# The samples' paged-cache attention as a third stream inside prompt attention

## Chip, cores and metric

One core of one Trainium2 chip. The metric is device time in microseconds of one execution, the median of three runs.

## The reference

One inference step of a two-layer decoder trunk: a gated-DeltaNet layer with a ConvFFN, then a multi-head latent attention (MLA) layer with a ConvFFN. The step serves a prompt of 1040 tokens (16 learned meta tokens and 1024 tokens) and eight samples with one new token each. The second layer keeps one shared latent key/value row of 256 numbers and one rotated positional key of 64 numbers per token. A prompt token attends causally to the prompt. A sample attends to its own 4096 cached tokens, which lie in pages of 128 tokens in a pool, and to its own new token:

```python
def latent_scores(q_lat, q_pe, c, k_rope):
    s = jnp.einsum('bqhr,bkr->bhqk', q_lat, c) + jnp.einsum('bqhd,bkd->bhqk', q_pe, k_rope)
    return s.astype(jnp.float32) * MLA_SCALE

def sample_attend(q_lat, q_pe, c, k_rope, c_past, k_past):
    ...
    s_past = latent_scores(q_lat, q_pe, c_past, k_past)
    ...
    prob = jax.nn.softmax(jnp.concatenate([s_past, s_new], axis=-1), axis=-1).astype(c.dtype)
    return (jnp.einsum('bhqk,bkr->bqhr', prob[..., :P], c_past)
            + jnp.einsum('bhqk,bkr->bqhr', prob[..., P:], c))
```

After attention each head's latent result is multiplied by `w_uv`, all heads go through the output projection `b_w_out`, and a norm and the last ConvFFN follow. There are eight heads; all data is float32.

## The kernel before

Activations lie transposed, with features on partitions and the 1048 tokens along the free dimension: the eight samples first, then the prompt, in chunks of 280, 384 and 384 columns (`CH`). Products of the trunk are taken three times over halves of a split float32 number (`mm3`, L226). Products written directly in float32 take two matmul records each in the profile.

Code is written as generators that yield a position. `merge` (L834) runs those of one stage in order of position, which gives the program order; the framework under it then settles, ahead of the run, the order of the instructions on each engine and on the DMA queue that SyncE issues (SP's queue), by program order and its own estimate of times. On the chip every queue runs strictly in that order, and an instruction that waits holds up what is behind it.

Three stages matter here.

**Latents** (to L1227). `lat_qa` makes `qah` and `qal`, the two halves of the low-rank query, with a row factor kept in `RQ`.

**Prompt attention** (L1230 to L1440). `merge` runs `attend` with one `heads_in` per head. Position h to h+1 is head h. `heads_in` loads and splits that head's weights and makes queries (`q_nope`, `q_rope`, scaled by `RQ` on VectorE, L1279), keys and values; it also makes the samples' query of that head, against transposed `w_uk` (L1261, L1289). `attend` takes nine blocks of 116 queries: `scores` writes to `sc` in PSUM (five products), VectorE masks and takes the maximum (L1365 to L1373), ScalarE takes the exponential (L1375), VectorE scales by the row sum (L1382). `mix` transposes the probabilities on TensorE (L1394), and products with the values `vt` collect in `po` (L1408), which rotates through two PSUM banks and is stored to `og_d` in DRAM.

**Cache attention and output projection** (L1443 to L1616). `merge` runs `cache_all` with `outp`. `cache_unit` runs 16 times, one unit for 2048 cached tokens of one sample. GpSimd gathers two `cg` tiles of 1 MB (L1468) and one `krt` tile (L1471) by indirect DMA. TensorE transposes the latents (L1487) and the positional keys (L1476) into PSUM, VectorE and ScalarE copy them out. Scores come from `ql` and `qr_s` as 32-column weights on four column tiles (L1493) and on 64-row tiles (L1497). Then the maximum (L1502), the exponential (L1506), transposes of the probabilities (L1510), products with `cg` (L1516) and a running rescale of `OS` (L1523 to L1531). `join` merges the partial results, adds the new token, and multiplies by `w_uv` (L1591) and by `b_w_out` for the samples (L1599). `outp` (L300) projects the prompt's columns.

## Time and profile before

| | us |
|---|---|
| median of three runs (lowest 3307.54, highest 3319.37) | 3309.26 |
| the profiled execution | 3314.68 |
| its span, first to last instruction | 3312.9 |
| prompt attention, with the last latents | 1770 to 2150 |
| cache attention, join, output projection | 2150 to 2490 |

The mean granted TensorE clock of the profiled execution is 0.975 of full speed. The page gives the share of the span in which each engine was busy and the chain of work that ended last. A stage is read from the table of stretches, an order from the timeline, a price from the groups of instructions by line and shape. A matmul's duration has a pipeline tail in it: the pace is the distance between starts.

### The profile page before, as it was taken

Reading aid. Unit: us, or ns where it says so; the run is one execution under the profiler, and the core shown is the slowest. Engines: PE = TensorE matmul, PEld = TensorE weight load, DVE = VectorE, ACT = ScalarE, POOL = GpSimd, SP = SyncE. Lnnn points to the kernel's source line nnn. Section 1 sums busy time; section 2 is a strip of 40 time slices with the busy share of each in tenths; the row PEclk is TensorE's granted clock in tenths of the full one; section 3 lists DMA queues with packets and bytes.
Section 4 is the critical chain, followed back from the end, with each engine's and each line's share of the span. In section 5 each row is a group of like instructions: output and inputs, shape, how many; then the busy total and the mean of one; then the engine's idle time right before and its main releaser. Section 6 shows DMA issues by size and latency. Waiting matters only on the chain.

```text
span 3312.9 us, 52527 instructions
## 1 busy us (share of the span) xinstructions
PE 3123.5 (94%) x20846; PEld 2884.2 (87%) x20846; DVE 2030.3 (61%) x4139; ACT 1254.9 (38%) x2541; POOL 862.2 (26%) x1013
## 2 busy tenths in 40 slices
PE   7999999999899999999978999999998999999997
PEld 6888888888799999999967888856678999999996
DVE  4777777766864555555576676544557355555556
ACT  4656555563433222222334444433224322222223
POOL 1433222210342222322342111111105332322322
PEclk9999999999899999999989999999998999999999
DMA  3222222235321111111121000354432111111111
GB/s 107 62 65 69 64 67 59 72 105 176 96 66 46 39 52 49 48 46 39 45 86 44 25 27 28 108 189 184 159 102 84 46 46 45 46 45 52 46 39 66
DMA packets 267650, 235.08 MB, mean 71 GB/s; under 512 B 57919, under 2 KB 246597, under 8 KB 263285
## 3 DMA queue, kind: packets, MB, share of 16 engines
q1 hardware_dynamic: 260224, 189.69, 19.7%
q0 software_dynamic: 6912, 41.95, 3.4%
q8 instruction: 164, 2.69, 0.3%
q14 instruction: 82, 0.66, 0.1%
q10 hardware_dynamic: 268, 0.09, 0.0%
HBM read 198.84 MB, written 33.40 MB: 70 GB/s over the span
## 4 chain that ended last, share of the span: by engine, by line
PE 76%; DVE 14%; DMA 3%; issue 3%; ACT 2%; POOL 1%; SPq 0%; ACTq 0%; POOLq 0%; DVEq 0%
PE fps L228 9%; PE fps L229 9%; PE fps L227 9%; PE fdn L228 5%; PE fdn L227 5%; PE fdn L229 5%; PE psu L227 2%; PE psu L229 2%; PE po L1408 2%; PE psu L228 2%; PE dscr L1493 2%; DVE acc L287 2%; PE psop L227 1%; DVE tm L658 1%; DVE xs L660 1%
## 5 line engine op out<-in xcount | busy, mean ns | idle before, releaser
L144 POOL TENSOR_TENSOR ws<-ws,vec 128x1024 f32<-128x1024 f32 (+1 forms) x127 | 249.5, 1965 | 424.3 <-DMA ws<-in_f_w_up_dram 210.1
L228 PE MATMUL fps<-xfl,wh 128*128 128x384 f32 (+1 forms) x1056 | 343.7, 326 | 8.2 <-POOL xfl L295 8.1
L227 PE MATMUL fps<-xfh,wh 128*128 128x384 f32 (+1 forms) x1056 | 341.8, 324 | 8.0 <-ACT xfh L293 7.0
L228 PE MATMUL fps<-xbl,wh 128*128 128x384 f32 (+1 forms) x1056 | 343.6, 325 | 4.8 <-POOL xbl L295 4.7
L227 PE MATMUL fps<-xbh,wh 128*128 128x384 f32 (+1 forms) x1056 | 341.6, 324 | 1.1 <-ACT xbh L293 0.5
L229 PE MATMUL fps<-xfh,wl 128*128 128x384 f32 (+1 forms) x1056 | 342.4, 324 | 0.0
L229 PE MATMUL fps<-xbh,wl 128*128 128x384 f32 (+1 forms) x1056 | 341.2, 323 | 0.0
L966 DVE TENSOR_TENSOR fu<-fps,RS 128x384 f32<-128x384 f32 x176 | 98.0, 557 | 386.6 <-PE fps L229 386.1
L151 ACT CAST wh<-ws 128x1024 fp32r<-128x1024 f32 (+1 forms) x144 | 148.0, 1027 | 491.6 <-PE fps L228 373.8
L227 PE MATMUL fdn<-gh,dh 128*128 128x384 f32 (+1 forms) x960 | 315.2, 328 | 0.0
L228 PE MATMUL fdn<-gl,dh 128*128 128x384 f32 (+1 forms) x960 | 311.6, 325 | 0.0
L229 PE MATMUL fdn<-gh,dl 128*128 128x384 f32 (+1 forms) x960 | 308.6, 321 | 0.0
L1044 DVE TENSOR_TENSOR acc<-acc,fdn 128x384 f32<-128x384 f32 (+1 forms) x432 | 216.7, 514 | 108.8 <-PE fdn L229 108.0
L227 PE MATMUL psu<-xah,wh 128*128 128x384 f32 (+1 forms) x768 | 261.8, 341 | 9.5 <-ACT u L533 5.1
L228 PE MATMUL psu<-xal,wh 128*128 128x384 f32 (+1 forms) x768 | 260.0, 339 | 0.7 <-DVE xal L223 0.7
L229 PE MATMUL psu<-xah,wl 128*128 128x384 f32 (+1 forms) x768 | 259.0, 337 | 0.7 <-DVE wl L152 0.7
L975 DVE SCALAR_TENSOR_TENSOR fy<-fu,fcv,fy 128x1064 f32<-128x1064 f32 x176 | 238.6, 1357 | 7.6 <-ACT fy L973 7.3
L152 DVE TENSOR_TENSOR wl<-ws,wh 128x1024 fp32r<-128x1024 f32 (+1 forms) x144 | 173.6, 1206 | 71.3 <-ACT wh L151 71.1
L228 PEld LDWEIGHTS fps<-xfl,wh 128*128 128x128 f32 x1056 | 200.7, 190 | 10.8 <-POOL xfl L295 10.5
L227 PEld LDWEIGHTS fps<-xfh,wh 128*128 128x128 f32 x1056 | 200.3, 190 | 9.4 <-ACT xfh L293 7.9
L228 PEld LDWEIGHTS fps<-xbl,wh 128*128 128x128 f32 x1056 | 200.5, 190 | 6.9 <-POOL xbl L295 6.5
L227 PEld LDWEIGHTS fps<-xbh,wh 128*128 128x128 f32 x1056 | 200.2, 190 | 1.7 <-ACT xbh L293 0.9
(963 smaller groups left out, 7856.1 us busy)
## 6 DMA issues: line engine op xcount, KB each, us to landing
ws<-in_f_w_up_dram SPq DMA_DIRECT2D x88, 512.0 KB
ds<-in_f_w_down_dram SPq DMA_DIRECT2D x44, 512.0 KB
ws<-in_a_w_in_dram SPq DMA_DIRECT2D x32, 512.0 KB
xt<-in_x_prompt_dram SPq DMA_DIRECT2D x16, 512.0 KB
of<-og_d SPq DMA_DIRECT2D x32, 192.0 KB
xr<-x_d SPq DMA_DIRECT2D x16, 384.0 KB
GC<-gcd SPq DMA_DIRECT2D x24, 174.0 KB
Ss<-in_state_delta_S_dram SPq DMA_DIRECT2D x8, 512.0 KB
```

Of the source, the lines that this page charges most:

```text
L144: G.tensor_tensor(st, st, bc(fo, [P, kt, m]), op=ALU.mult)
L151: A.copy(hi, st)
L152: V.tensor_tensor(lo, st, hi, op=ALU.subtract)
L227: PE.matmul(ps, wh, ah, start=start, stop=False)
L228: PE.matmul(ps, wh, al, start=False, stop=False)
L229: PE.matmul(ps, wl, ah, start=False, stop=stop)
L287: V.scalar_tensor_tensor(a_[:, k + j, :], a_[:, k + j, :], vc(wname, k + j), res[j], op0=ALU.mult, op1=ALU.add)
L966: V.tensor_tensor(u[:, 18 + t0:18 + t0 + n], ps[:, :n], RS[:, t0:t0 + n], op=ALU.mult)
L975: V.scalar_tensor_tensor(y, u[:, j:j + LW], fcv[:, l, j, tl:tl + 1], y, op0=ALU.mult, op1=ALU.add)
L1044: V.tensor_tensor(acc[c][:, m, :], acc[c][:, m, :], ps[:, :n], op=ALU.add)
L1408: PE.matmul(po[:, :nq], vt[:kk, kb, P * (h % 2):P * (h % 2) + P], pT[:kk, j, :nq], start=(kb == 0), stop=(kb == i))
L1493: PE.matmul(sc[32 * j:32 * j + 32, :], ql[:, k, b, :], cT[:, j, :], start=(k == 0), stop=False, tile_position=(0, 32 * j))
```

## The change

The whole cache attention and the join move into the merge of prompt attention, as further streams; the output projection runs alone behind it and takes the samples' columns too, since the join now stores them to `og_d`.

- A unit is now 1024 cached tokens (32 units), spread evenly over positions `C0` = 0.15 to `C1` = 7.2, each with its steps at 0, 0.1, 0.25, 1.1, 1.35 and 1.55 unit lengths. Unit n+2 is gathered after unit n's last product: there are two `cg` buffers, two `cT`, two `cB`.
- No TensorE transposes of the cache. VectorE transposes 32 by 32 blocks (`turned`), SyncE stores the tile to DRAM and reads it back in four transfers, each into 32 partitions.
- Scores have 256 columns each instead of 512; the positional part contracts over all 128 partitions, with half of `qr_s` zero.
- The samples' queries are made once for all heads (`sample_queries`), with the queries as 32-column weights.
- `RQ` is folded into `qah` and `qal` in `lat_qa`; VectorE's product L1279 goes, and the subtraction for `qnl` moves from GpSimd to VectorE.
- The scaling of the probabilities (L1382) moves from VectorE to GpSimd.
- Fewer buffers: P 3 to 2, pT 4 to 3; `po` becomes four slots of one PSUM bank; the scores and products of the cache share one bank (`halves`).

The core of the diff:

```diff
-PTB = 4
+PTB = 3
+PB = 2
+C0 = 0.15
+C1 = 7.2
...
         def lat_qa(c):
             t0, n = CH[c]
-            stat(kst, [acc[c][:, 3 + m, :] for m in range(3)], n, RQ[:, t0:t0 + n], QL)
+            r = utile("rqa")
+            stat(kst, [acc[c][:, 3 + m, :] for m in range(3)], n, r[:, :n], QL)
             for m in range(3):
                 a = acc[c][:, 3 + m, :]
-                A.activation(qah[:, m, t0:t0 + n], a, AF.Copy, scale=vc("b_qa", m))
-                V.scalar_tensor_tensor(qal[:, m, t0:t0 + n], a, vc("b_qa", m), qah[:, m, t0:t0 + n], op0=ALU.mult, op1=ALU.subtract)
+                V.scalar_tensor_tensor(a, a, vc("b_qa", m), r[:, :n], op0=ALU.mult, op1=ALU.mult)
+                A.copy(qah[:, m, t0:t0 + n], a)
+                G.tensor_tensor(qal[:, m, t0:t0 + n], a, qah[:, m, t0:t0 + n], op=ALU.subtract)
...
-                u = atile("qu")
-                V.tensor_tensor(u[:, :n], ps[:, :n], RQ[:, t0:t0 + n], op=ALU.mult)
-                return u[:, :n], t0, n
+                return ps[:, :n], t0, n
...
-                G.tensor_tensor(hd["qnl"][:, t0:t0 + n], u, hd["qnh"][:, t0:t0 + n], op=ALU.subtract)
+                V.tensor_tensor(hd["qnl"][:, t0:t0 + n], ps, hd["qnh"][:, t0:t0 + n], op=ALU.subtract)
...
-                V.tensor_scalar(pp[:nq, :nk], pp[:nq, :nk], ls[:nq, 0:1], None, op0=ALU.mult)
+                G.tensor_scalar(pp[:nq, :nk], pp[:nq, :nk], ls[:nq, 0:1], None, op0=ALU.mult)
...
+        def fetch(n):
+            if n < 4 * NS:
+                fetched[n] = big("cg")
+                G.indirect_dma_start(fetched[n], None, crows, offset(n))
...
+        def turned(src, tmp, nb, nm):
+
+            V.transpose(grid(tmp, nb, 8, 32), src.rearrange("p i (b r) -> p b i r", r=32))
+            d = dp.tile([P, nb, 256], F32, tag=nm, name=nm, bufs=2)
+            SP.dma_start(d, grid(tmp, nb, 256))
+            return d.rearrange("(q r) b c -> b r q c", q=4)
+
+        def cache_unit(n, at_):
+
+            b, g = divmod(n, 4)
+            yield at_(0.0)
...
+            src = turned(grid(fetched.pop(("r", n)), 8, ROPE), cpg.tile([P, 1024], F32, tag="cB", name="krB")[:, :512], 2, "krd")
+            for i in range(2):
+                for f in range(2):
+                    SP.dma_start(krT[64 * f + 32 * i:64 * f + 32 * i + 32, :].rearrange("r (q c) -> r q c", q=2), src[i, :, f:4:2, :])
+            fetch_r(n + 1)
+            cT = []
+            for k in range(2):
+                yield at_(0.1 + 0.15 * k)
+                t = cmat("cT")
+                cT.append(grid(t, 4, 256))
+                src = turned(c8[:, :, P * k:P * k + P], cpg.tile([P, 1024], F32, tag="cB", name="cB"), 4, "cBd")
                 for i in range(4):
-                    PE.transpose(pt[:, P * i:P * i + P], krt[:, P * (4 * gg + i):P * (4 * gg + i) + P], ident)
-                V.tensor_copy(krT[:, gg, :], pt)
...
+                    SP.dma_start(cT[k][32 * i:32 * i + 32], src[i])
+            yield at_(1.1)
+            sc = halves[:, 0, :]
             for k in range(2):
...
                 for j in range(4):
-                    PE.matmul(sc[32 * j:32 * j + 32, :], ql[:, k, b, :], cT[:, j, :], start=(k == 0), stop=False,
+                    PE.matmul(sc[32 * j:32 * j + 32, :], ql[:, k, b, :], cT[k][:, :, 64 * j:64 * j + 64], start=(k == 0), stop=False,
                               tile_position=(0, 32 * j))
...
+            for f in range(2):
+                for j in range(4):
+                    PE.matmul(sc4[32 * j:32 * j + 32, f:4:2, :], qr_s[:, f, b, :], kr4[:, :, 64 * j:64 * j + 64],
+                              start=False, stop=(f == 1), tile_position=(0, 32 * j))
...
+            yield at_(1.55)
+            pv = halves[:, 1, :]
+            for c in range(2):
                 for j in range(4):
...
+                    PE.matmul(pv[32 * j:32 * j + 32, :], pT[:, c, 32 * j:32 * j + 32], c8[:, 2 * j + c, :],
+                              start=(c == 0), stop=(c == 1), tile_position=(0, 32 * j))
+            fetch(n + 2)
...
+        merge(attend(), *[heads_in(h, h - HA, h - HB) for h in range(H)], sample_queries(),
+              *[cache_unit(n, at_(n, None)) for n in range(4 * NS)], join(at_(C1 + 0.2, 0.45)))
...
-        merge(cache_all(0, CA), outp(I["b_w_out"][0], og_d, groups, ogp, 0.05, 1.0, True, NS, 6))
+        merge(outp(I["b_w_out"][0], og_d, groups, ogp, 0.0, 1.0, True, 0, 6))
```

## Rows read from the trace of the kernel before

**Rows 1.** The page: busy engines (section 1), the chain that ended last (section 4)

```profile
PE 3123.5 (94%) x20846; PEld 2884.2 (87%) x20846; DVE 2030.3 (61%) x4139; ACT 1254.9 (38%) x2541; POOL 862.2 (26%) x1013
...
PE 76%; DVE 14%; DMA 3%; issue 3%; ACT 2%; POOL 1%; SPq 0%; ACTq 0%; POOLq 0%; DVEq 0%
```

**Rows 2.** Stretches: start:end, length, busy us per engine, clock, DMA share, GB/s

```profile
1770.00:2150.00 380.00, 354.01 (x2524) 331.64 (x2525) 251.61 (x686) 181.94 (x442) 43.91 (x43) 0.99 0.14 45
1850.00:2090.00 240.00, 227.11 (x1668) 214.50 (x1667) 163.70 (x458) 115.60 (x286) 24.99 (x25) 1.00 0.09 27
2150.00:2400.00 250.00, 247.56 (x1896) 151.68 (x1895) 117.31 (x255) 77.75 (x163) 39.77 (x43) 0.99 0.50 181
2400.00:2450.00 50.00, 46.60 (x201) 30.57 (x200) 13.82 (x24) 6.92 (x9) 4.02 (x4) 0.86 0.41 128
2450.00:2490.00 40.00, 38.49 (x242) 35.49 (x240) 33.35 (x53) 18.50 (x29) 3.37 (x2) 1.00 0.26 72
```

**Rows 3.** TensorE's waits, longest first: prompt attention (first row), cache attention (its only one)

```profile
PE vps L1325 <- ACT vt L1328: 5.4, 4, 1.4
...
PE dct__22305 L1487 <- ACT cT L1491: 2.1, 1, 2.1
```

**Rows 4.** Timeline of TensorE through one cache unit: start us, us, instruction, xcount

```profile
2232.53 1.90 PE L1493 MATMUL dscr<-cT,ql 128*32 128x512 f32 x8
2234.36 0.66 PE L1487 MATMUL dct__23026<-ident,cg 128*128 128x128 f32 x4
...
2238.16 1.06 PE L1497 MATMUL dscr<-krT,qr_s 64*32 64x512 f32 x8
...
2241.17 0.60 PE L1510 MATMUL dpt<-ident,p 128*128 128x128 f32 x4
2241.61 0.93 PE L1476 MATMUL dkt<-ident,krt 128*128 128x128 f32 x7
2242.47 1.93 PE L1516 MATMUL pv<-cg,dpT 128*32 128x256 f32 x32
```

**Rows 5.** Timeline: pace of the output projection, 384 and 272 columns

```profile
2452.64 0.33 PE L227 MATMUL psop<-ogh,wx 128*128 128x384 f32 x1
2452.81 0.33 PE L228 MATMUL psop<-ogl,wx 128*128 128x384 f32 x1
...
2480.54 0.28 PE L228 MATMUL psop<-ogl,wx 128*128 128x272 f32 x1
2480.66 0.29 PE L229 MATMUL psop<-ogh,wx 128*128 128x272 f32 x1
```

**Rows 6.** One line: duration ns, first and last start; groups: busy us, mean ns

```profile
L227 PE MATMUL sc<-knh,qnh x112: 213/372/465, 1809.1 to 2136.5; 128*116 128x348 f32 x24, 128*116 128x464 f32 x24, 128*116 128x290 f32 x16, 128*116 128x406 f32 x16
...
L668 DVE STREAM_TRANSPOSE Tt<-X x8: 458/459/466, 157.5 to 748.6; 32x288 f32<-32x288 f32 x8
...
L1502 DVE TENSOR_REDUCE MX<-dscr 128x1 f32<-128x512 f32 x8 | 5.5, 692 | 18.1 <-PE dscr L1497 18.1
...
L1382 DVE TENSOR_SCALAR P<-P,ls 116x116 f32<-116x116 f32 (+8 forms) x72 | 39.0, 542 | 2.0
...
L1285 POOL TENSOR_TENSOR qnl<-qu,qnh 128x384 fp32r<-128x384 f32 x14 | 14.4, 1025 | 55.3 <-ACT qnh L1284 55.3
```

**Rows 7.** DMA: queues (packets, MB, share), a gather's landing, chain pieces, SP's issue (ns)

```profile
q1 hardware_dynamic: 260224, 189.69, 19.7%
q0 software_dynamic: 6912, 41.95, 3.4%
...
cg<-in_cache_kv_latent_dram,idx POOLq DMA_INDIRECT x32, 7.1
...
320.22 3.46 DMA vr<-vd
...
155.77 1.75 DMA X<-xd
...
L666 SPq DMA_DIRECT2D X<-xd x32: 308/418/456, 155.8 to 745.0; - x32
```

382 lines of the change are left out of this document (222 added, 160 removed).

## Prediction

> **What bounds the kernel now.** I read the page first. TensorE is busy for 94% of the span and makes 76% of the chain that ended last [rows 1]: work that leaves TensorE shortens the kernel, work put on other engines is free while it hides. Second, the table of stretches, for the stages that the change touches [rows 2]. In prompt attention (1770 to 2150) TensorE is busy 354 of 380 us, VectorE 252, ScalarE 182, GpSimd 44, and in its steady part DMA only 9%. From 2150 to 2400 TensorE is busy 247.6 of 250 us although it issues cache transposes that compute nothing. Third, TensorE's waits: the longest in prompt attention sums to 5.4 us, the cache stage has one of 2.1 us [rows 3]. So both stages run at TensorE's pace, one after the other, and VectorE, GpSimd and DMA have room in the first.
>
> **What leaves.** The stretch 2150 to 2490 lasts 340 us [rows 2]. It holds 16 cache units, the join, and the output projection. From the starts of the rows of one unit [rows 4]: four transposes take 2241.61 - 2241.17 = 0.44 us; the unit has 32 of latents (3.5 us), 8 of keys (0.9) and 4 of probabilities (0.4); the latent scores take 2234.36 - 2232.53 = 1.83 us twice (3.7), the positional scores 1.0, the products with the cache 1.9. That is 11.4 us, times 16 is 182 us. The output projection alone has 8 heads x 8 tiles x 3 products: 384 products of 384 columns at 0.173 us and 192 of 272 columns at 0.125 us [rows 5], 90 us. The remaining 68 us are the join with its low clock (0.86 in that stretch), hand-overs and small transposes. After the change the stretch is the projection alone: 90 us and 10 for start and hand-over (an estimate: two weight loads of 3.5 us, the landing in [rows 7], and their split). **Saved: 340 - 100 = 240 us.**
>
> **What TensorE gets in prompt attention.** Per new unit: latent scores are 16 records of 256 columns, the same shape as the products with the cache, whose 32 records took 1.93 us [rows 4]: 0.97 us. The positional scores are 16 records of 128 columns, between half of that and all of it: 0.7. Two transposes 0.25, products 0.97. **2.9 us x 32 = 93 us.** From below, 2.6 (positional scores at half); from above 4.1, if the scores keep the pace of the old ones (8 records of 512 columns in 1.83 us, which is 1.83 for the same columns): 83 to 131 us.
>
> The rows disagree here: the old latent scores and the products with the cache both use 32-column weights, yet per streamed column the first pay twice as much. [...]
>
> The samples' queries for all heads: about 8 us by the same paces (18 records of 512 columns, 24 transposes, 16 records of 256), against 32 short products and 16 transposes removed, about 6; the join 6 us. Together +8. `lat_qa` puts a norm, a copy and a subtraction between the last latents and the first queries; head 0 makes its keys first, so I take nothing, 5 us if uncovered. So at TensorE's pace attention grows by 93 + 8 = 101 us, and the balance is **101 - 240 = -139 us**.
>
> **What the other engines get.** VectorE's 32 by 32 transpose took 459 ns for 288 columns [rows 6]: 1.6 ns a column as an upper price, 1.35 by the 692 ns of a 512-column maximum. I take 1.4 us for 1024 columns. A unit has two of these and one of 512, 3.5 us, a maximum 0.4, and by an estimate 1.4 for the rescale of `os` (256 columns at 1.35 ns) and seven one-column steps: 5.3 us x 32 = 170 us. Off VectorE go the scaling of P, 39 us [rows 6], and the product with `RQ`, 36 instructions of 280 or 384 columns, at 1.35 ns a column 17; on it comes the query's low half, 24 of these, 11. 252 + 170 - 56 + 11 = 377 us in a stage of 480 to 530: not the bound, but each transpose is a 1.4 us block in front of the masks and maxima that TensorE waits for.
>
> GpSimd takes the scaling of P: 72 steps over 580 columns on average. Its nearest row is 1025 ns for 384 columns with two inputs [rows 6], so at most 1.5 us each, at least VectorE's 0.54. Cover: the next block's scores are issued before the transposes that need P. Without that cover it costs up to 72 us. It also issues 64 gathers. The single `po` bank makes the next block's product wait for a copy of 0.3 us, mostly behind the next scores: nothing taken, 20 us at most.
>
> **What sets the pace of a unit.** Units are spread over 7.05 heads. Eight heads lasted from the first scores at 1809 [rows 6] to 2150, 42.5 us each, so at TensorE's pace the 32 units have 7.05 x 42.5 + 93 + 3 = 396 us, **12.4 us each**. Two things may be slower.
>
> First, DMA. The gathers moved 41.95 MB in 3.4% of the span on all engines [rows 7], 113 us, 3.5 us per new unit. The same bytes are now also stored and read back: at the gathers' rate 7.0 us, at the SP queue's mean rate (189.69 MB in 19.7%, 653 us) 9.0. With attention's own 9% that is 11.6 to 13.6 us of DMA in a unit of 12.4.
>
> Second, the loop through the two `cg` buffers, which must close within two units, 24.8 us. Gather 7.1 us, two block transposes 2.8, store 3.5 (like `vr`, 512 KB), four issues of 0.42, landing 1.75 [rows 7], scores 1.7, maximum 0.6, exponential 0.6, transposes and copy 0.6, products 0.97: 21.3 us. It leaves 3.5 us for eleven hand-overs to queues that are busy. An estimate of 0.55 us each, half an instruction of VectorE's, makes 27.4, or 13.7 per unit. I take **13.8 us**: both limits lie near it. Excess over TensorE's pace: 1.4 x 32 = 45 us, in which TensorE stands in attention.
>
> **Sum:** -240 + 101 + 45 = -94 us. The profiled execution took 3314.7 us (span 3312.9), 5.4 above the median of 3309.3; I apply the difference to the median: **3215 us**.
>
> **The rivals.**
>
> *TensorE stays the bound.* If gathers land early and hand-overs are short, a unit takes 12.4 us: 3309 - 139 = 3170, or 3160 with the low price of a unit. For it: almost no waits now [rows 3]. Against: a loop with 3.5 us of slack.
>
> *Reading back is slow.* The four read-backs of a tile go to 32 partitions each; no row shows a transfer of that size into so few. If that halves their rate, 3.5 to 4.5 us of DMA per unit come on top, 15.1 to 18.1. At 16 us per unit: 3215 + 2.2 x 32 = 3285. [...]
>
> *SP's queue locks step: slower than before.* SP must not read a tile back before its store has landed. If the queue's order puts each read-back directly behind its store, SP stands still meanwhile: 0.42 + 3.5 + 4 x 0.42 = 5.6 us per tile, three tiles per unit 16.8, and 1 us for the heads' own loads and stores: 17.8 us. Then 3215 + 4 x 32 = 3343. It decides from about 17.3 us a unit on, where the kernel is 0.5% slower. For it: three dependent stores per unit on one queue. Against: the order is settled ahead, so other tiles' stores can stand between a store and its read-back, and old waits of SP did not reach TensorE [rows 3].
>
> **How the numbers follow.** My forecast (3190 to 3250) 0.50; TensorE bound 0.17; slow read-back (3250 to 3310) 0.19; SP in step 0.14. What a measurement of this kernel can tell from no change is about 0.5%, 16.5 us: faster below 3293, slower above 3326. The read-back case straddles the first limit: 0.12 of it is faster, 0.07 the same; SP in step splits into 0.02 the same and 0.12 slower. So faster 0.79, same 0.09, slower 0.12. The range runs from the middle of TensorE's case to that of the read-back, 3165 to 3300; it leaves out about 0.2.
>
> **What would show it.** The stretch between attention and the last ConvFFN should be 95 to 110 us. Attention should last 480 to 500 us if TensorE bounds it, about 525 by my forecast, 600 with slow read-back, above 640 with SP in step. A unit's TensorE records should take 2.6 to 4.1 us. DMA should be busy 80% or more in attention. TensorE's waits there should be for `cT` and for VectorE's maxima. I am wrong if the wait before the scores of the cache is small and attention is still long (then GpSimd's scaling or VectorE's order is the cause), or if the projection needs much more than 110 us alone.

## The result and the profile after

| | before | after |
|---|---|---|
| median, us (4 runs each, same session) | 3308.40 (3304.62 to 3319.37) | 3427.62 (3422.24 to 3439.65) |
| the profiled execution, us | 3314.68 | 3431.25 |
| its span, us | 3312.9 | 3429.5 |
| mean granted TensorE clock | 0.975 | 0.947 |

The ratio is 1.036, 95% interval 1.0321 to 1.0398: slower, by 119 us. The forecast was 3215, the range 3165 to 3300. The prediction was wrong in its sign.

The share of busy time is read first, as in [rows 1]: TensorE is busy for 32 us less, and for a smaller share of a longer span (90% for 94%).

```profile
PE 3091.8 (90%) x20818; PEld 2863.2 (83%) x20818; DVE 2046.0 (60%) x4164; ACT 1232.5 (36%) x2585; POOL 1029.4 (30%) x1138
```

The table of stretches of the kernel after says where (start:end, length, busy us of PE, PEld, DVE, ACT and POOL, granted clock, DMA share, GB/s). It answers [rows 2]: prompt attention with the cache units, its steady part, the output projection alone, and the passage to the ConvFFN.

```profile
1770.00:2476.00 706.00, 547.12 (x4236) 429.14 (x4235) 371.18 (x946) 223.28 (x617) 246.45 (x210) 0.86 0.66 207
1850.00:2440.00 590.00, 451.56 (x3594) 353.84 (x3593) 302.13 (x773) 174.04 (x495) 208.85 (x180) 0.85 0.70 221
2476.00:2577.00 101.00, 95.39 (x576) 91.75 (x575) 42.70 (x76) 26.51 (x52) 5.70 (x3) 0.98 0.24 73
2577.00:2645.00 68.00, 44.17 (x202) 35.88 (x201) 55.61 (x67) 31.18 (x46) 28.27 (x18) 0.77 0.37 109
```

From the starts of single instructions, first scores of attention to its last product with the values, then to the last product of the projection, then to the first twenty-fourth of the ConvFFN's products:

| stretch | before | after | difference | predicted |
|---|---|---|---|---|
| attention | 1809 to 2148, 339 us | 1814 to 2476, 662 us | +323 | +146 |
| behind it, to the end of the projection | 339 us | 101 us | -238 | -240 |
| passage to the ConvFFN | 44 us | 68 us | +23 | 0 |

The saving came as summed. What attention got was more than twice what the sum allowed it, and 23 us came on top that no step had named. Together these are 108 of the 117 us by which the profiled span grew; 5 more lie ahead of the first scores and the rest behind the passage. TensorE's waits in the steady part of attention (us in total, times, longest us) answer [rows 3], where the longest sum was 5.4 us:

```profile
PE dpt L1598 <- ACT p L1583: 80.1, 27, 6.3
PE scpv L1570 <- DMA cT<-cBd: 24.1, 9, 5.0
PE dpt L1598 <- issue: 13.6, 3, 6.4
PE sc L229 <- ACT P L1369: 8.5, 8, 3.7
```

The latent scores of the 32 units (duration ns, first and last start) run from 1851.9 to 2441.3, so a unit takes 589.4 / 31 = **19.0 us**, where the prediction took 13.8:

```profile
L1570 PE MATMUL scpv<-cT,ql x512: 376/379/637, 1851.9 to 2441.3; 128*32 128x256 f32 x171
```

### The profile page after: what moved, and what is told of

Its sections match the earlier page's. It is cut to its first block, busy times and chain, and to the rows that moved or that the text cites. A ratio compares the mean times of both kernels' runs of the same rounds, so it can differ in the third digit from the quotient of the medians.

```text
span 3429.5 us, 53714 instructions
## 1 busy us (share of the span) xinstructions
PE 3091.8 (90%) x20818; PEld 2863.2 (83%) x20818; DVE 2046.0 (60%) x4164; ACT 1232.5 (36%) x2585; POOL 1029.4 (30%) x1138
## 5 line engine op out<-in xcount | busy, mean ns | idle before, releaser
L972 POOL COPY fcs<-fu 128x8 f32<-128x8 f32 x88 | 86.1, 978 | 430.3 <-DVE fu L965 430.1
L229 PEld LDWEIGHTS fps<-xbh,wh 128*128 128x128 f32 x1056 | 201.1, 191 | 11.6 <-ACT xbh L295 9.9
```

The costliest lines, as they stand in the source:

```text
L229: PE.matmul(ps, wh, ah, start=start, stop=False)
L972: G.tensor_copy(cs[:, slot, 0:8], us[:, :, 2])
```

## The experiments

Each kernel is the changed one with the edit shown. The table has for each the length of attention (first scores to last product of the prompt), the pace of a unit (first to last latent scores, by 31), and from a stretch of its steady part (for the two kernels without units, from all of attention) the granted clock, a mean of stretches at full speed and at half of it (the clock records of the kernel after have these two values alone, 55 stretches of each), and the share of the DMA engines. I compare lengths of attention rather than single times, since the stage's start moved between 1794 and 1822 us from kernel to kernel, mostly with the code ahead of it unchanged. Each length is from one profiled execution, and a row for which the text gives no ratio rests on that one execution alone. The four executions of the changed kernel lie 17 us apart, so a difference of some 15 us between two rows is not told by them.

An edit can do more than its lines say, since the framework settles the order of each queue anew for every kernel. From the first store of a turned tile to the last read-back SP issues 523 transfers in the kernel after. By the order of starts in the traces all of them stand in the same order in p_on_vector, about 519 in filler, 483 in three_room, 414 in late, 304 in bounce_beside, 284 in quarter and 113 in free_back.

| kernel | attention, us | unit, us | clock | DMA share | time, us |
|---|---|---|---|---|---|
| before | 339 | | 1.00 | .09 | 3308.4 |
| after | 662 | 19.0 | .85 | .70 | 3427.6 |
| p_on_vector | 663 | 19.1 | .86 | .71 | 3428.4 |
| no_units | 406 | | .96 | .14 | 3171.9 |
| no_units_pv | 363 | | .98 | .15 | 3130.1 |
| no_bounce | 501 | 13.6 | .99 | .36 | 3269.2 |
| no_bounce_pv | 485 | 13.3 | .98 | .36 | 3233.0 |
| no_bounce3_pv | 469 | 12.9 | 1.00 | .38 | 3229.0 |
| wide_back | 587 | 16.4 | .91 | .74 | 3347.7 |
| by_store | 703 | 20.1 | .82 | .68 | 3469.2 |
| free_back | 650 | 18.5 | .86 | .72 | 3422.3 |
| bounce_beside | 640 | 17.8 | .86 | .74 | 3409.2 |
| three | 764 | 22.1 | .78 | .60 | 3527.0 |
| three_room | 655 | 18.5 | .86 | .75 | 3418.4 |
| three_room_pv | 651 | 18.6 | .85 | .76 | 3420.1 |
| late | 673 | 19.2 | .86 | .69 | 3431.7 |
| filler | 706 | 20.1 | .90 | .65 | 3472.0 |
| quarter | 535 | 14.8 | .96 | .49 | 3296.5 |
| pe_turn3 | 550 | 15.1 | .99 | .32 | 3313.1 |
| hybrid | 531 | 14.7 | .99 | .54 | 3302.7 |

### What the parts cost

**p_on_vector**, GpSimd's scaling undone:

```diff
-                G.tensor_scalar(pp[:nq, :nk], pp[:nq, :nk], ls[:nq, 0:1], None, op0=ALU.mult)
+                V.tensor_scalar(pp[:nq, :nk], pp[:nq, :nk], ls[:nq, 0:1], None, op0=ALU.mult)
```

> The changed kernel with one edit: the probabilities of prompt attention are scaled on VectorE again (71 times .54 us by the trace of before) and not on GpSimd (71 times 1.76 us by the trace of the changed kernel). GpSimd theory (the slow scaling stands in the chain of scores, maxima, exponentials and transposes, and GpSimd also issues the gathers): attention falls from 662 us by 40 to 100 us and the time to 3330 to 3390 us. Latency theory (each cache unit is a loop through DRAM, 38.8 us per two units): the scaling lies beside that loop, attention stays at 640 to 670 us and the time at 3405 to 3435 us. VectorE theory (VectorE's own order holds up the units): 38 us more VectorE work, the time 3430 to 3470 us.

Measured: 3428.44 us, ratio to before 1.0358 (1.0324 to 1.0393); the changed kernel had 1.036. With SP's order unchanged this is a clean test. The GpSimd theory falls: nothing of the loss hangs on the scaling as long as the units go at 19 us.

**no_units** and **no_units_pv**, without the cache units, then with the scaling on VectorE too:

```diff
-              *[cache_unit(n, at_(n, None)) for n in range(4 * NS)], join(at_(C1 + 0.2, 0.45)))
+              join(at_(C1 + 0.2, 0.45)))
```

> The changed kernel without the 32 cache units; the samples' queries and the closing join remain and work on zeros, so the samples' attention over the cache is left out. It prices what else the change did to the attention stage: scaling on GpSimd, one bank for the products, fewer buffers, the folded query norm. By the prediction's sum: attention 339 us plus 8 us of TensorE work, 340 to 360 us, the time 3110 to 3135 us. GpSimd theory: the scaling of 1.76 us costs 20 to 70 us by itself, attention 365 to 415 us, the time 3135 to 3190 us. The passage from the output projection to the ConvFFN, 44 us before and 68 after, stays at 68 us if it has lost the cache work as cover, and falls back to 44 us if the units' leftovers (the clock, late stores) lengthen it.

> The changed kernel without the 32 cache units (left out as before, the samples' queries and the join remain) and with the probabilities scaled on VectorE. Without units attention was 406 us against 339 in the kernel before and 347 by the prediction's sum; TensorE's waits for the scaling on GpSimd were 27.6 us of it and its granted clock .96 against .99. If the scaling on GpSimd is most of the rest: attention 360 to 380 us, the time 3125 to 3145 us. If it is the samples' queries, the single product bank or the fewer buffers: attention 395 to 410 us, the time 3160 to 3175 us.

Attention took 406 us, 67 more than before, and 363 with the scaling on VectorE. Here the scaling does show, first in TensorE's longest group of waits in no_units (us in total, times, longest), then in the scaling's own group there (busy us, mean ns, idle before it).

```profile
PE ptr L1388 <- POOL P L1376: 27.6, 27, 3.1
```
```profile
L1376 POOL TENSOR_SCALAR P<-P,ls 116x116 f32<-116x116 f32 (+8 forms) x72 | 127.1, 1765 | 222.9 <-DVE ls L1375 161.2 <-PE sc L1355 22.3 <-PE po L1403 21.2
```

So 67 us are 43 of scaling and 24 of the rest (samples' queries, join, folded norm, fewer buffers), for which the sum had 8. The 43 us are not additive: with the units they were gone. The passage to the ConvFFN, from the end of the projection to the last `fps`, stays equally long without units (767 us in the kernel after and in no_units, 742 before), so its 23 us are not a leftover of the units.

**no_bounce** and **no_bounce_pv**, without the way through DRAM (the same for the rope rows; the exchange of the 32-partition groups is left out), then with the scaling on VectorE:

```diff
-                src = turned(c8[:, :, P * k:P * k + P], cpg.tile([P, 1024], F32, tag="cB", name="cB"), 4, "cBd")
-                for i in range(4):
-                    SP.dma_start(cT[k][32 * i:32 * i + 32], src[i])
+                V.transpose(grid(t, 4, 8, 32), c8[:, :, P * k:P * k + P].rearrange("p i (b r) -> p b i r", r=32))
```

> The changed kernel without the way through DRAM: VectorE turns the 32x32 blocks straight into the operands of the scores, and the stores and read-backs are gone. It leaves out the exchange of 32-partition groups, so the samples' scores are those of permuted rows. All of VectorE's, TensorE's and ScalarE's instructions remain. Latency or transfer theory (the round trip, 17.7 of a loop of 38.8 us, or its bytes set the pace): the loop falls to 22 to 25 us, a unit to 11 to 13 us, attention from 662 us to 440 to 500 us, the time to 3210 to 3270 us. GpSimd or order theory (TensorE stands before the transposes of the samples' probabilities, put too early, and its clock falls): attention stays above 580 us, the time above 3345 us.

> The version without the way through DRAM (permuted rows, as before) and with the prompt's probabilities scaled on VectorE. With the scaling on GpSimd it had 501 us of attention; without units the place of the scaling was worth 43 us (406 to 363), with the way through DRAM nothing. If that scaling counts as soon as TensorE's pace sets the end: 455 to 475 us, the time 3220 to 3245 us. If a unit's loop sets the pace here too: 490 to 505 us, the time 3255 to 3275 us.

Attention 501 and 485 us: the first is at the upper end of what the latency or transfer theory expected, the second lies between its two expectations. The stretch of no_bounce beside that of the kernel after is the study's main reading: about as many TensorE records (3518 for 3594), 170 us less.

```profile
1850.00:2270.00 420.00, 384.07 (x3518) 310.57 (x3517) 285.87 (x752) 170.22 (x485) 203.28 (x176) 0.99 0.36 115
```

TensorE is idle 420 - 384 = 36 us here and 590 - 452 = 138 us there: 102 us of the difference. The other 67 us are in its busy time: 76 records more, some 8 us, and 59 us by which the records are slower, at a granted clock of .85 and not .99 (126 ns and 109 ns of busy time a record). The units themselves cost 501 - 406 = 95 us, or 485 - 363 = 122 us where the scaling hides nothing; the prediction had 93.

So the 323 us are: 24 rest, 43 scaling, 95 units, **161 the way through DRAM**. The split depends on the order in which the parts are taken away: with the scaling on VectorE throughout it is 24 rest, 122 units, 178 the way through DRAM (663 - 485), and nothing for the scaling. Either way the largest part is the one whose term in the prediction was 45.

### Why the way through DRAM costs 161 us

**wide_back**, one read-back into 128 partitions for four into 32 (the exchange of groups left out):

```diff
-                for i in range(4):
-                    SP.dma_start(cT[k][32 * i:32 * i + 32], src[i])
+                SP.dma_start(cT[k], src)
```

> The changed kernel with the way through DRAM, but each turned tile is read back by one transfer into 128 partitions with rows of 4 KB (2 KB for the rope rows), not by four into 32 partitions each with rows of 1 KB. Same bytes, 3 transfers a unit for 12; the exchange of the 32-partition groups is left out, so the samples' scores are those of permuted rows. Transfer theory (narrow read-backs and 1 KB packets take the time): the DMA share in attention falls from .70 to under .55 and a unit from 19.2 to 14 to 16 us, attention from 662 to 510 to 570 us, the time to 3280 to 3340 us. Latency theory (steps behind each other, whatever the shape): only some 9 issues on the SP queue and their waits go, 1 to 2.5 us of a loop of 38.8 us; attention 620 to 655 us, the time 3385 to 3425 us.

**by_store**, the exchange in the store, so that the stores are narrow and the read-back wide:

```diff
-            SP.dma_start(d, grid(tmp, nb, 256))
+            for q in range(4):
+                SP.dma_start(d[:, q, :].rearrange("(b r) c -> r b c", b=nb), grid(tmp, nb, 256)[32 * q:32 * q + 32])
```

> The changed kernel with the exchange of the 32-partition groups moved from the read-back to the store: four stores from 32 partitions with pieces of 1 KB for each turned latent tile, and one read-back into 128 partitions with rows of 4 KB (the rope rows: four stores, two read-backs). Same bytes, same result, 14 transfers a unit for 15. If narrow read-backs into 32 partitions make the round trip long, it falls by most of what the one-transfer version gave (75 us of attention): attention 585 to 615 us, the time 3350 to 3385 us. If it was their number, or the 1 KB pieces on whichever side, little changes: attention 640 to 675 us, the time 3405 to 3440 us.

wide_back, wide on both sides, gained 75 us of attention, between its two expectations, but with the DMA share up to .74, not down; by_store, wide on the read-back's side alone, lost 41. Both expectations of by_store were missed upward. So the narrow read-back as such is not the cause: attention took 662 us with the narrow side on the read-back, 703 with it on the store and 587 with neither narrow. What of it costs is not told apart, since narrow transfers are also more transfers, in pieces of 1 KB and not 4 KB.

**free_back**, read-backs from a tile stored once:

```diff
-            return d.rearrange("(q r) b c -> b r q c", q=4)
+            return old[nm].rearrange("(q r) b c -> b r q c", q=4)
```

> The changed kernel in which the read-backs, same shapes, bytes and count, take a DRAM tile that was stored once ahead of the stage; the stores stay, but no read-back waits for one. The samples' scores are those of a fixed tile, so the samples' result is left out. Latency theory (the steps behind each other in the loop, not the bytes, set the pace; the share of the DMA engines, .70 of 19.2 us, is 13.5 us a unit): a unit falls to 13.5 to 15.5 us, attention from 662 us to 500 to 560 us, the time to 3270 to 3330 us, and the DMA share rises to .85 or more. Rate theory (the narrow read-backs go no faster than this): the unit stays at 18 us or more, attention above 630 us, the time above 3395 us.

Only 12 us. The two longest groups of TensorE's waits in it tell why it is a poor test. SP's order is mostly another one, and TensorE now waited 46 us (24.5 here and 21.9 at L1318) for ScalarE's copies of the heads' weights; ScalarE itself waited 30 us for these weights to land:

```profile
PE dpt L1604 <- ACT p L1589: 65.3, 19, 7.2
PE qps L229 <- ACT wh L153: 24.5, 4, 14.6
```

**three** and **three_room**, a third buffer for the gathered rows; three makes room by single buffers (`cB`, `p`, `dpT`), three_room by loading the rope tables in chunks, by two buffers and not three for the prompt's transposed probabilities, and by keeping the samples' own latent rows in DRAM; **three_room_pv** has the scaling on VectorE too:

```diff
-            return cpg.tile([P, 8 * KVL], F32, tag="cg", name=nm)
+            return cpg.tile([P, 8 * KVL], F32, tag="cg", name=nm, bufs=3)
...
-            fetch(n + 2)
+            fetch(n + 3)
```

and, for the room in three_room, tables in place of `cosq` and `sinq`:

```diff
+    def rope_tables(c):
+        t0, n = CH[c]
+        for x in ("cos", "sin"):
+            tab[x] = mp.tile([P, 384], F32, tag=x, name=x)
+            SP.dma_start(tab[x][:, :n], I[f"c_{x}q"][:, t0:t0 + n])
```

> The changed kernel with three buffers for the gathered cache rows and the gather of unit n+3 behind unit n's products, in place of two and n+2; room for it from one buffer each, not two, for the turned tile, the probabilities and their transposes, and two, not three, for the transposes of prompt attention. Latency theory: the loop of 38.8 us, longer by some 3 us for the single buffers, now spans three units: 13 to 15 us a unit, bound by DMA or TensorE, attention 500 to 570 us, the time 3270 to 3340 us. Rate theory: nothing to gain, attention 650 us or more, the time 3415 us or more. SP-queue rival (SP takes its instructions in order and stands at each store until VectorE has turned): a third buffer does not help, attention above 620 us.

> The changed kernel with three buffers for the gathered rows and the gather of unit n+3 behind unit n's products; both turned tiles and all other buffers of the units remain double. Room comes from the rope tables, loaded in chunks of 384 columns ahead of each use, from two buffers, not three, for the prompt's transposed probabilities, and from the samples' own latent rows, kept in DRAM until the join. Same result. Loop theory: 38.8 us over three units is 13 us, so a unit takes 13 to 15.5 us (TensorE's 13.1, the transfers' 13.5), attention 500 to 570 us, the time 3270 to 3340 us. Transfer theory or SP's order: 18 us a unit or more, attention above 630 us, the time above 3395 us.

> The same with the prompt's probabilities scaled on VectorE. Loop theory: with TensorE's pace near, the scaling counts (43 us without units, 17 us without the way through DRAM), attention 480 to 550 us, the time 3245 to 3320 us. Transfer theory or SP's order: no difference to the scaling on GpSimd, the time above 3390 us.

three was 102 us of attention slower, ratio 1.0635 (1.0589 to 1.0682): with one `cB` the next turn waits for the store, and SP stood 138 us for stores to land (35 in the kernel after). It tells the price of single buffers and nothing of the loop. three_room is the cleaner test, although it loads the tables again during attention, and the loop theory fails it: 18.5 us a unit, ratio 1.0315 (1.0258 to 1.0372). From a gather's issue to the end of its products a unit took 38 us in the kernel after and 55 us here (medians over the units). The third buffer only made the line longer.

**bounce_beside**, scores from the tile that VectorE turned, with all stores and read-backs kept into a tile that nothing reads:

```diff
-                src = turned(c8[:, :, P * k:P * k + P], cpg.tile([P, 1024], F32, tag="cB", name="cB"), 4, "cBd")
+                V.transpose(grid(t, 4, 8, 32), c8[:, :, P * k:P * k + P].rearrange("p i (b r) -> p b i r", r=32))
+                src = spare(t, 4, "cBd")
+                cx = grid(cpg.tile([P, 1024], F32, tag="cB", name="cX"), 4, 256)
                 for i in range(4):
-                    SP.dma_start(cT[k][32 * i:32 * i + 32], src[i])
+                    SP.dma_start(cx[32 * i:32 * i + 32], src[i])
```

> The version whose scores take the tile that VectorE has turned (permuted rows, as in the version without the way through DRAM), but with all stores and read-backs kept, in shapes, bytes, number and queue, into a tile that nothing reads. Loop theory (the steps of a unit behind each other set the pace): as without the way through DRAM, attention 500 to 540 us, the time 3268 to 3305 us. Transfer theory (bytes, narrow read-backs or SP's order set the pace, whoever waits): attention 600 to 665 us, the time 3365 to 3430 us.

Attention 640 us: the transfers cost nearly as much when no score waits for their data. Its steady stretch, then TensorE's two longest groups of waits in it, and ScalarE's wait for such weights:

```profile
1850.00:2400.00 550.00, 419.77 (x3586) 336.23 (x3587) 292.89 (x767) 173.55 (x490) 207.58 (x180) 0.86 0.74 228
```
```profile
PE vps L1318 <- ACT wh L153: 28.9, 3, 12.0
PE qps L229 <- ACT wh L153: 27.6, 2, 16.0
...
ACT wh L153 <- DMA ws<-in_b_w_q_b_dram: 15.2, 2, 13.5
```

TensorE has no wait for a read-back left, and it is idle 130 us all the same, 56 of them for ScalarE's copies of the heads' weights. These weights are loaded by the same SP queue, but for their landing ScalarE waited only 17 us, 13.5 of them once. Ahead of the other copies it stood at instructions of its own order that waited for VectorE. What one removes at one wait comes up at another.

**quarter**, the same transfers in number, queue and dependences, each with a quarter of the columns (the scores read that quarter four times):

```diff
-            SP.dma_start(d, grid(tmp, nb, 256))
+            SP.dma_start(d, tmp[:, :64 * nb])
...
-                    SP.dma_start(cT[k][32 * i:32 * i + 32], src[i])
+                    SP.dma_start(cT[k][32 * i:32 * i + 32, 0:1, :], src[:, i:i + 1, :])
```

> The changed kernel with a quarter of the bytes on the way through DRAM: same stores and read-backs in number, order, queue and waits, each with one quarter of the columns; the scores read that quarter four times over (as many columns for TensorE), so the samples' scores are those of other rows. Transfer theory (what the stores and read-backs take of the DMA engines holds up the gathers, the weight loads and each other): the DMA share falls from .70 to .40 to .50, attention from 662 us to 500 to 560 us, the time to 3265 to 3330 us. Queue theory (15 transfers a unit on SP's one queue, .44 us each to issue, with landings behind each other, whatever their size): attention 600 to 655 us, the time 3365 to 3425 us.

Attention 535 us, as the transfer theory had it. Taking away three quarters of the bytes gave back 127 of the 161 us; the number of the transfers, which stayed, and the last quarter of the bytes hold the other 34. Two things went along with the bytes. The order did not stay, as the expectation says it would: about 284 of SP's 523 transfers stand as before. And the read-backs have a quarter of the 1 KB pieces. The order by itself is an unlikely cause, since bounce_beside and free_back have other orders too, with all the bytes, and stayed at 640 and 650 us; no run holds it fixed.

```profile
1850.00:2300.00 450.00, 398.93 (x3497) 316.06 (x3496) 285.86 (x750) 169.64 (x483) 200.03 (x174) 0.96 0.49 153
```

By the landing events of the trace, a latent store landed 2.8 us behind its issue in the kernel after and 1.7 in quarter, a latent read-back 3.2 and 1.8 (medians). How busy the DMA engines were in 40 slices of each steady stretch, and their packets, kernel after first, then quarter (a digit is a tenth):

```profile
DMA  4777854787687676875586776758655678587867
...
DMA packets 75952, 130.27 MB, mean 221 GB/s; under 512 B 10673, under 2 KB 57931, under 8 KB 72063
```
```profile
DMA  3634543753454553552555345626452555445546
...
DMA packets 46854, 68.78 MB, mean 153 GB/s; under 512 B 10384, under 2 KB 40544, under 8 KB 42966
```

In no slice of the kernel after, 14.8 us long, do the engines reach nine tenths. Within the slices the work comes in bursts: by the packet records all 16 engines are at work for 45% of the time and none for 15%.

**late**, the samples' transposes and products a quarter of a unit later, and **filler**, useless products ahead of those transposes:

```diff
-            yield at_(1.35)
+            yield at_(1.6)
...
-            yield at_(1.55)
+            yield at_(1.8)
```

> The changed kernel with the samples' transposes of probabilities and products put a quarter of a unit later into TensorE's order (1.6 and 1.8 of a unit, not 1.35 and 1.55). If TensorE's standing ahead of these transposes is itself the loss (order theory): it goes, 65 us, and attention falls to 590 to 620 us, the time to 3355 to 3385 us. Loop theory (gather, turning, round trip, scores, products and the next gather into the same buffer are one chain of 38.8 us for two units): the chain gets longer by what is put between, up to 3 us of 38.8; TensorE stands for the read-backs instead, attention 655 to 710 us, the time 3420 to 3475 us.

```diff
+            for _ in range(12):
+                PE.matmul(halves[:, 1, :], cTh[:, 0, 0:P], cTh[:, 0, 0:256], start=True, stop=True)
```

> The changed kernel with 12 matrix products of 256 columns, which nothing uses, ahead of the transposes of the samples' probabilities in each unit, where TensorE stands 65 to 82 us in all: 384 products, at .11 to .17 us each 1.3 to 2 us a unit, 42 to 64 us in all. Loop theory (TensorE stands because the unit's steps follow each other through several engines; the fall of its granted clock to .85 is a consequence that makes the rest of its work longer): the products fall into time that was idle, the granted clock rises, attention stays at 640 to 665 us and the time at 3405 to 3430 us, less if the clock's part weighs. TensorE theory (its work at its order sets the pace): attention grows by the products, 700 to 730 us, the time 3470 to 3495 us.

late changed nothing that can be told (ratio 1.0364, interval 1.0327 to 1.0402): the wait ahead of the transposes stayed, so a quarter of a unit's delay does not remove it. filler's attention and time (706 us, 3472 us) came out as the TensorE theory had them, but not by its mechanism, since it did not fill what it was meant to fill. Its products write the bank whose scores the exponential reads, and they themselves waited for it:

```profile
PE scpv L1596 <- ACT p L1583: 95.5, 30, 6.3
```

They came behind the wait, not into it. Their 384 products took 71 us from start to start, .185 us each and 2.2 us a unit, and attention grew by 44, with the mean granted clock up from .85 to .90. So a step put into a unit's chain lengthened the stage by three fifths of itself, although TensorE was idle for a fifth of the time.

### Other ways to turn the cache

**pe_turn3**, all turning on TensorE, three gather buffers, the scaling on VectorE:

```diff
+                for i in range(2):
+                    pt = mtile("ct")
+                    for j in range(4):
+                        PE.transpose(pt[:, P * j:P * j + P], c8[:, 4 * i + j, P * k:P * k + P], ident)
+                    (V.tensor_copy if i else A.copy)(t[:, 512 * i:512 * i + 512], pt)
```

> Another form of the change, same result: the cache is turned by TensorE (20 transposes a unit, .157 us each by the trace of before, 3.1 us) and copied from the accumulators by ScalarE and VectorE, so no DRAM round trip; three buffers for the gathered rows in the room of the turned tiles; prompt probabilities scaled on VectorE. Without units and with that scaling attention was 363 us. TensorE theory: 363 + 32 x (3.0 + 2.5 to 3.1) = 539 to 558 us of attention if TensorE is kept at work, the time 3305 to 3327 us, level with the kernel before. If the loop of a unit still sets the pace (gather 6 to 8 us, five evictions of .6 us, scores and products behind the prompt's work): 580 us or more, the time 3350 us or more.

**hybrid**, the first 128 latent columns and the rope columns by TensorE, the other 128 by VectorE and DRAM, two gather buffers, the scaling on VectorE:

```diff
+                if k == 0:
...
+                    continue
                 src = turned(c8[:, :, P * k:P * k + P], cpg.tile([P, 1024], F32, tag="cB", name="cB"), 4, "cBd")
```

> Another form of the change, same result: of each unit's rows TensorE turns the first 128 latent columns and the rope columns (12 transposes), VectorE and DRAM the other 128 latent columns (one store, four read-backs, 5 transfers for 15); two buffers for the gathered rows; the prompt's probabilities scaled on VectorE. With all 20 transposes on TensorE attention was 550 us, 5.8 us a unit above the 363 us without units. TensorE theory: 8 transposes less, 32 x 8 x .157 = 40 us, attention 505 to 530 us, the time 3265 to 3295 us, faster than both kernels. If what is left of the way through DRAM still holds up the units: attention 545 to 600 us, the time 3310 to 3365 us.

**no_bounce3_pv**, the edits of no_bounce, p_on_vector and three's two lines for the third buffer together:

> The version without the way through DRAM, scaling on VectorE, and three buffers for the gathered rows in the room of the turned tiles. With two it had 485 us of attention. If TensorE set that pace: 478 to 490 us, the time 3225 to 3250 us. If the loop through two buffers still did: 455 to 472 us, the time 3200 to 3225 us.

pe_turn3: 550 us of attention as summed, 3313.1 us, ratio 1.0001 (0.998 to 1.0022), level with the kernel before. hybrid: 531 us, 3302.71 us (3279.09 to 3309.04, ten runs), ratio **0.9944** (0.9924 to 0.9964): against 1.036 for the changed kernel, and half a percent ahead of the one before. It missed both ranges of the TensorE theory, by 1 us of attention and 8 us of time. Their steady stretches, pe_turn3 first: TensorE is at work for 97% and 95%, at a granted clock of .99, and hybrid hides a DMA share of .54.

```profile
1850.00:2320.00 470.00, 458.02 (x4181) 377.33 (x4184) 276.35 (x791) 221.29 (x581) 95.42 (x116) 0.99 0.32 104
```
```profile
1850.00:2320.00 470.00, 446.44 (x4042) 361.30 (x4044) 294.74 (x818) 212.51 (x572) 97.05 (x119) 0.99 0.54 180
```

no_bounce3_pv gained 16 us of attention on no_bounce_pv, but only 4 of time: its stage began 11 us later. So where the transfers are few, the loop through two buffers may be felt, which single executions do not settle; where they are many, three_room shows that it is not what sets the pace.

## Why the prediction was wrong, step by step

**What leaves: right.** 340 - 100 = 240; measured 238, the projection alone 101 us.

**TensorE's work in a unit: right.** 93 us were taken for 32 units, 83 to 131 as bounds. One unit of no_bounce at full clock, from TensorE's timeline (start us, us), answers [rows 4]:

```profile
2095.78 1.07 PE L1565 MATMUL scpv<-cT,ql 128*32 128x256 f32 x16
2096.67 0.62 PE L1570 MATMUL scpv<-RS,qr_s 128*32 128x128 f32 x16
2100.11 0.44 PE L1593 MATMUL dpt<-ident,p 128*128 128x128 f32 x2
2101.01 1.07 PE L1599 MATMUL scpv<-cg,dpT 128*32 128x256 f32 x16
```

The latent scores take 2096.67 - 2095.78 = 0.89 us where 0.97 was taken and 1.83 was the upper bound, and by the starts of all four steps a unit has some 2.6 us, 85 us for 32. Attention grew by 95 us with the units (122 with the scaling on VectorE), so 10 to 37 of these are not their work on TensorE. Of the two prices of the scores, by the products' row and by the old scores' row, the lower holds; why the old scores paid twice as much per column, no run shows.

**Other TensorE work in attention: too low.** 8 us were taken for queries and join; it is 24 without the units. The scaling's bound was too low too: at most 1.5 us each were allowed, the rows show 1.77. Its upper bound of 72 us was not reached, its value of nothing held with the units.

**VectorE's transposes: right.** 1.4 us for 1024 columns were taken; 1.23 us in the kernel after, .70 for 512 (busy us, mean ns, idle before and what ended it), beside the scaling's group, for [rows 6]:

```profile
L1537 DVE STREAM_TRANSPOSE cB<-cg 128x1024 f32<-128x1024 f32 x61 | 74.0, 1231 | 24.5 <-DMA cg<-in_cache_kv_latent_dram,idx 23.0 <-DMA cT<-cBd 1.4
L1376 POOL TENSOR_SCALAR P<-P,ls 116x580 f32<-116x580 f32 (+8 forms) x64 | 113.4, 1772 | 126.0 <-DVE ls L1375 96.0 <-PE sc L1355 11.0 <-ACT pT L1392 7.6
```

**The pace of a unit: the step that failed.** The prediction took 11.6 to 13.6 us of DMA a unit and a loop of 27.4 us, and from both a pace of 13.8, with 45 us of excess. The pace was 19.0, and the way through DRAM cost 161 us. The amount of DMA was right: a share of .70 of 19.0 us is 13.3 us of all engines. What was wrong is to read it as a limit that is met at a share of 1, where a unit could go at 13.3; the forecast of 80% or more was not reached either. With all bytes on the way through DRAM the share stood between .68 and .76 in nine kernels, whether there were two or three gather buffers, four read-backs or one, and whether or not anything waited for them (three and filler, with more steps behind each other in a unit, had .60 and .65); the pace of the nine was 16.4 to 20.1 us. By .70 to .76 the same 13.3 us would have been 17.5 to 19.0. (A share is the work of a unit over its pace, so it restates the slow pace and does not by itself show a ceiling.) Below a share of .5 (no_bounce, pe_turn3, quarter) or at .54 (hybrid) a unit went at 12.9 to 15.1, near TensorE's pace.

The loop was mis-sized as well: 38.8 us from a gather to the next gather but one (median), not 27.4, with read-backs landing at 3.2 us, where 1.75 was taken. But three_room shows that this loop is a consequence: given a third buffer it grew.

**The clock: a step that is missing.** The 45 us of extra pace were counted as TensorE standing still. Standing still was 102 us of the difference to no_bounce, and 59 us more were the slower records at a mean granted clock of .85. By the stretches of the table a TensorE that was idle for 3 to 9% of the time had a clock of .98 to 1.00, for 11 to 13% .96 (quarter, no_units), for 17% .91 (wide_back), for 22 to 25% .85 or .86, for 27% .82 (by_store) and for 32% .78 (three); filler, which put useless work on TensorE, raised it to .90 at 22%. So idle time of TensorE cost about one and a half times its length here, 161 us for 102.

**The passage behind the projection: a step that is missing.** Before, the passage lay partly beside the cache work's end. The first ConvFFN product started 1.4 us behind the last of the projection; now it is 11.9 us, and TensorE waits there for the norm's square sums and for the split of the rows (22 us in the rows below, where the kernel before had 5 at the split and 3 more):

```profile
PE fps L229 <- ACT xbh L295: 8.9, 3, 5.4
PE fps L230 <- POOL xbl L297: 8.4, 4, 2.6
PE st_ps L267 <- DVE s L261: 5.1, 3, 3.5
```

That the projection's overlap was lost is read from the traces of both kernels; no run put it back.

**The rivals.** *TensorE stays the bound* fell. *SP in step* forecast attention above 640 us and a slower kernel, and both came; its mechanism did not. SP stood at stores 35 us in 590, not 5 us at each of three a unit, as SP's own waits in the steady part show, and in quarter SP stood longer at stores (24.4 us at the latents', 35.5 at the rope rows') and attention was 127 us shorter. In the kernel after SP stood longest for VectorE:

```profile
SPq L1539 <- DVE cB L1537: 90.4, 20, 11.6
SPq L1413 <- DVE oT L1410: 78.2, 12, 10.6
SPq L1539 <- DVE sc L1359: 38.8, 8, 9.2
SPq L1565 <- DMA cBd<-cB: 34.9, 27, 4.1
```

A slow queue by its order, and not by its stores, is not ruled out, since no run gives SP another order and leaves the rest.

*The sign of being wrong* came: the wait before the scores of the cache was small, 24.1 us, and attention was long. Of the two causes that the prediction named for it, GpSimd's scaling is ruled out by p_on_vector. To VectorE's order TensorE's longest wait does lead, since the exponential that it waits for waited for VectorE (first row, kernel after). But no_bounce keeps all of VectorE's instructions, and there TensorE's wait is 12.7 us (second row). So VectorE's order alone does not make it; that it hands on what the transfers delay is likely and not shown.

```profile
ACT p L1583 <- DVE nm L1587: 132.4, 21, 11.1
...
PE dpt L1593 <- ACT p L1578: 12.7, 12, 2.3
```

*Slow read-back* forecast 16 us a unit by more DMA work for narrow transfers. (Its sum gives 3285; the range's upper end, 3300, is called its middle and does not come out of that sum. The measured time lies above both.) The DMA work was as in the main forecast. In the trace's packet records a piece of 1 KB took 59 ns on the mean in the kernel after, one of 4 KB 187 ns in wide_back, 26% more per byte, not double. That narrow read-backs go at half rate, and so the 3.5 to 4.5 us of DMA a unit on which this rival's time and the upper end of the range rest, was the author's supposition; no run shows it, and the runs showed the 26% and the 13.3 us of DMA in a unit instead. If narrow read-backs alone were the cause, wide ones should gain by themselves; by_store, with wide read-backs and narrow stores, was slower by 41 us. That does not rule a price of narrow transfers out, since the narrowness moved to the other side.

**What stays open.** Shown are the amounts: 161 us for the way through DRAM, 127 of them gone with three quarters of the bytes, 22 with the waits for the read data, 7 with a third gather buffer. That it is the bytes, and not the number of pieces or the order that changed with them, is argued and not shown. Nor is it shown what keeps the DMA engines at .68 to .76. The bursts in the packet records, the price of filler and the weight waits of bounce_beside point to ordered queues that pass each other's delays on: SP's, on which stores, read-backs, weights and results stand in one line (by the trace of the kernel after its 1234 transfers start in the order of the program), VectorE's (so do its 4164 instructions), and those of ScalarE and TensorE. No run separated these; a second queue for the read-backs was not tried.

## What to carry to other kernels

Work that left a busy TensorE for the DMA queues was hidden here at a DMA share of .54 (hybrid) and not at .70 (the kernel after), so do not size the traffic against all of the engines' time, and count idle time on TensorE with more than its length: here 102 us of standing came with 59 us of slower records, at a clock of .85 and not .99. When a wait is long, take the bytes, the waiting and the number of transfers away one at a time, and compare the orders of the queues before you call the rest equal: the longest wait that the profile names moved here from the exponential (80 us in the kernel after) to the weights (two groups, 56 us together, in bounce_beside) while the stage stayed about as long (662 and 640 us). And split the load: in this kernel a third of the transfers on DRAM and the rest as transposes beat all on either, if only by half a percent (ratios to before: hybrid .9944, pe_turn3 1.0001, the kernel after 1.036).

## What was not expected of the hardware

- GpSimd scales 580 columns on average by a per-partition factor in 1.77 us (no_units and the kernel after), VectorE the same 72 steps in .52 us (no_units_pv).
- VectorE's 32 by 32 transpose takes 1.23 us for 1024 columns, 1.2 ns a column; it had 1.6 in the narrow row of before [rows 6].
- With all stores, gathers and read-backs together the 16 DMA engines gave 208 GB/s at a share of .68 (by_store) and 254 at .74 (wide_back).
- A product into one half of a PSUM bank waited for the exponential that reads the other half (filler, 95.5 us in 30 waits). Whether the chip or the program's own order asks for it, no run tells.
